# Instance norm on one core: statistics per tile instead of per four tiles, VectorE in program order, six data buffers instead of eleven

## The chip, the core and the metric

The kernel runs on one core of a Trainium2 chip. The metric is the device time of one execution in microseconds (us), lower is better. Each kernel has several timed executions; I quote their median and range. All profiled executions told here are "fast", with the clock granted in full (1.00). A profile also gives a span, from the first to the last work on the core, which is some 1.7 us less than the time of the same execution (1263.8 and 1265.47 us in the changed kernel).

Engine names in the profile: PE is TensorE, PEld its weight loads, DVE is VectorE, ACT is ScalarE, POOL is GpSimd, SP is SyncE; SPq and ACTq are the sequencers that issue DMAs.

## The reference

```python
# x: (8, 64, 32, 64, 64) float32, eps = 1e-5
mean = np.mean(x, axis=(2, 3, 4), keepdims=True)
var  = np.var(x, axis=(2, 3, 4), keepdims=True)
return (x - mean) / np.sqrt(var + eps)
```

There are 512 instances of 131,072 elements. Every element is read once and written once: 268.4 MB in, 268.4 MB out.

## The kernel before

A tile is 128 partitions x 4096 elements of float32, 2 MB in the profile's count (2048 KB), and holds four instances of 32 partitions each; there are 128 tiles. Per tile: a load on SP's queue, eight `bn_stats` and one `bn_aggr` on VectorE. Per batch of T = 4 tiles: a matmul with the selector `sel` sums the 32 partitions of each instance, ScalarE and VectorE make 1/std and -mean/std of them, a matmul with `sel2` spreads the two numbers over the partitions again. Then ScalarE normalises each tile in place and issues its store.

```python
T = 4
data_pool = ctx.enter_context(tc.tile_pool(name="data", bufs=11))
...
for b in range(NB):
    stats = stats_pool.tile([P, T, 2], fp32, name="stats")
    for ti in range(T):
        in_t = data_pool.tile([P, FT], fp32, name="in_t")
        nc.sync.dma_start(out=in_t, in_=x_v[t])
        for s in range(NS):                                  # NS = 8
            nc.vector.bn_stats(out=bnst[:, s, :], in_=in_t[:, s * BS : (s + 1) * BS])
        nc.vector.bn_aggr(out=stats[:, ti, :], in_=bnst)
    ...   # square, add, matmul, scale on ACT, variance, sqrt on ACT, reciprocal,
    ...   # product, matmul, copy to bcast: once for the four tiles
    for ti in range(T):
        nc.scalar.activation(out=in_t, in_=in_t, func=AF.Identity,
                             bias=bcast[:, ti, 1:2], scale=bcast[:, ti, 0:1])
        nc.scalar.dma_start(out=out_v[t], in_=in_t)
```

No engine has a prescribed order: a scheduler arranges each engine's instructions when the kernel is built.

## Time and profile before

| | before |
|---|---|
| time, median (range, runs) | 1317.3 us (1315.9 to 1319.3, 13 runs) |
| span of the profiled execution | 1316.0 us |
| bytes moved, mean rate | 537.05 MB, 408 GB/s |
| rate in undisturbed stretches | 429 to 433 GB/s |
| busy: DVE, ACT | 53%, 38% |

The first parts of the prediction show and read the main lines.

```profile
q14 instruction: 18, 0.15, 0.0%
q8 instruction: 1, 0.02, 0.0%
...
in_t<-in_x_dram SPq DMA_DIRECT2D x128, 2048.0 KB, 16.9
out_dram<-in_t ACTq DMA_DIRECT2D x128, 2048.0 KB, 22.8
```

Instruction traffic looks like nothing: 0.17 MB of 537.

### The profile page before, as it was taken

The page shows a single profiled execution, that of the slowest core. Times are in us where ns is not written, and L with a number is a line of the kernel's source. Part 1 is how long each engine was busy: PE and PEld are TensorE (multiplying, and loading weights), DVE is VectorE, ACT ScalarE, POOL GpSimd, SP SyncE. Part 2 cuts the span into 40 slices and gives each one's busy share as a digit, 9 for nine tenths or more (in the row PEclk, how much of TensorE's full clock was granted, in tenths as well). Part 3 has the DMA queues.
Part 4 walks back from the last instruction along what each step waited for, and adds up shares of the span by engine and source line. Part 5 has one row for each costly group of instructions (what it writes and reads, how often), then busy time and mean ns, then how long its engine had stood idle before and what let it go on. Part 6 is the DMA issues. An engine that isn't in the chain of part 4 may idle for free.

```text
span 1316.0 us, 2530 instructions
## 1 busy us (share of the span) xinstructions
PE 22.7 (2%) x128; PEld 18.4 (1%) x128; DVE 692.6 (53%) x1383; ACT 495.2 (38%) x194; POOL 0.8 (0%) x6
## 2 busy tenths in 40 slices
PE   0000000000000000000000000000000000000000
PEld 0000000000000000000000000000000000000000
DVE  7775546454464545645455454554635546455430
ACT  0431904409054080530805318053180631706345
POOL 0000000000000000000000000000000000000000
DMA  9999999999999999999999999999999999999979
GB/s 396 422 432 429 372 431 395 419 431 380 432 390 421 432 385 432 377 429 430 378 431 385 431 424 385 432 373 432 419 394 432 376 431 408 400 430 373 431 327 399
DMA packets 36883, 537.05 MB, mean 408 GB/s; under 512 B 4096, under 2 KB 4096, under 8 KB 4096
## 3 DMA queue, kind: packets, MB, share of 16 engines
q1 hardware_dynamic: 18432, 268.44, 49.0%
q10 hardware_dynamic: 18432, 268.44, 48.6%
q14 instruction: 18, 0.15, 0.0%
q8 instruction: 1, 0.02, 0.0%
HBM read 268.44 MB, written 268.44 MB: 408 GB/s over the span
## 4 chain that ended last, share of the span: by engine, by line
DMA 60%; ACT 14%; issue 14%; DVE 9%; ACTq 1%; PE 1%; SPq 0%
DMA out_dram<-in_t 38%; DMA in_t<-in_x_dram 22%; ACT in_t L171 14%; DVE bnst L101 7%; ACTq L178 1%; PE psum_b L158 1%; DVE stats L104 1%; ACT std_t L138 0%; DVE bcast L166 0%; DVE bsrc L147 0%; DVE bsrc L148 0%; DVE var_t L135 0%; DVE nm L126 0%; SPq L97 0%; DVE sq_tmp L106 0%
## 5 line engine op out<-in xcount | busy, mean ns | idle before, releaser
L101 DVE BATCH_NORM_STATS2 bnst<-in_t 128x6 f32<-128x512 f32 x1024 | 619.3, 677 | 554.0 <-DMA in_t<-in_x_dram 553.9
L171 ACT ACTIVATE in_t<-in_t,bcast 128x4096 f32<-128x4096 f32 x128 | 479.5, 3793 | 40.3 <-ACT in_t L171 20.3
L123 ACT ACTIVATE sc<-psum_s 4x8 f32<-4x8 f32 x32 | 5.3, 166 | 603.6 <-PE psum_s L114 502.9
L138 ACT ACTIVATE std_t<-var_t,eps_t 4x4 f32<-4x4 f32 x32 | 7.9, 289 | 161.3 <-DVE var_t L135 161.3
L104 DVE BATCH_NORM_AGGREGATE stats<-bnst 128x2 f32<-128x48 f32 x128 | 47.6, 372 | 4.4
L114 PE MATMUL psum_s<-stats,sel 128*4 128x8 f32 x64 | 6.3, 172 | 1067.6 <-DVE stats L109 997.5
L158 PE MATMUL psum_b<-bsrc,sel 4*128 4x8 f32 x64 | 16.4, 361 | 179.8 <-DVE bsrc L148 179.8
L114 PEld LDWEIGHTS psum_s<-stats,sel 128*4 128x4 f32 x64 | 3.6, 83 | 1069.9 <-issue 579.3
L158 PEld LDWEIGHTS psum_b<-bsrc,sel 4*128 4x128 f32 x64 | 14.8, 316 | 181.7 <-DVE bsrc L148 178.5
L166 DVE COPY bcast<-psum_b 128x8 f32<-128x8 f32 x32 | 5.3, 166 | 10.3 <-PE psum_b L158 10.0
L147 DVE RECIPROCAL bsrc<-std_t 4x4 f32<-4x4 f32 x32 | 5.2, 162 | 4.3 <-ACT std_t L138 4.3
L109 DVE TENSOR_TENSOR stats<-stats,sq_tmp 128x4 f32<-128x4 f32 x32 | 5.2, 163 | 1.1
L106 DVE TENSOR_TENSOR sq_tmp<-stats 128x4 f32<-128x4 f32 x32 | 5.2, 163 | 1.1
L148 DVE SCALAR_TENSOR_TENSOR bsrc<-sc,bsrc 4x4 f32<-4x4 f32 x32 | 4.8, 150 | 1.0
L135 DVE TENSOR_TENSOR var_t<-sc,nm 4x4 f32<-4x4 f32 x32 | 3.7, 146 | 0.0
L126 DVE SCALAR_TENSOR_TENSOR nm<-sc 4x4 f32<-4x4 f32 x32 | 2.7, 115 | 0.5 <-ACT sc L123 0.5
L123 ACT ACT_TABLE_LOAD x1 | 1.3, 1283 | 0.8 <-PEq L195 0.8
L138 ACT ACT_TABLE_LOAD x1 | 1.3, 1283 | 0.0
L58 DVE MEMSET sel<- 128x4 f32 x1 | 0.1, 62 | 0.9 <-PEq L195 0.9
L60 DVE MEMSET sel<- 32x1 f32 x4 | 0.2, 59 | 0.1
L64 POOL TENSOR_SCALAR_AFFINE_SELECT sel<-sel 4x128 f32<-4x128 f32 x1 | 0.3, 283 | 0.6 <-DVE sel L63 0.6
L73 POOL TENSOR_SCALAR_AFFINE_SELECT sel<-sel 4x128 f32<-4x128 f32 x1 | 0.3, 282 | 0.1
(6 smaller groups left out, 0.6 us busy)
## 6 DMA issues: line engine op xcount, KB each, us to landing
in_t<-in_x_dram SPq DMA_DIRECT2D x128, 2048.0 KB, 16.9
out_dram<-in_t ACTq DMA_DIRECT2D x128, 2048.0 KB, 22.8
```

Of the source, the lines that this page charges most:

```text
L101: nc.vector.bn_stats(out=bnst[:, s, :], in_=in_t[:, s * BS : (s + 1) * BS])
L104: nc.vector.bn_aggr(out=stats[:, ti, :], in_=bnst)
L106: nc.vector.tensor_mul(out=sq_tmp, in0=stats[:, :, 0], in1=stats[:, :, 0])
L109: nc.vector.tensor_add(out=stats[:, :, 1], in0=stats[:, :, 1], in1=sq_tmp)
L114: nc.tensor.matmul(out=psum_s, lhsT=sel, rhs=stats, start=True, stop=True,)
L123: nc.scalar.mul(out=sc1, in_=psum_s, mul=inv_PG)
L138: nc.scalar.activation(out=std_t, in_=var_t, func=AF.Sqrt, bias=eps_t[0:R, :], scale=1.0,)
L147: nc.vector.reciprocal(out=bsrc[:, :, 0], in_=std_t)
L158: nc.tensor.matmul(out=psum_b, lhsT=sel2, rhs=bsrc, start=True, stop=True,)
L166: nc.vector.tensor_copy(out=bcast, in_=psum_b)
L171: nc.scalar.activation(out=in_t, in_=in_t, func=AF.Identity, bias=bcast[:, ti, 1:2], scale=bcast[:, ti, 0:1],)
L178: nc.scalar.dma_start(out=out_v[t], in_=in_t)
```

## The change

The intent is to let every tile go out as soon as its own statistics are there. The small chain runs once per tile; VectorE keeps program order, tile after tile (a `LAG` of 0: tile t is finished before t+1 begins); and since a tile is held for a shorter time, six data buffers are to suffice. The division by 32 is folded into the constants. Core of the diff, with cuts:

```diff
-    T = 4
+    TAIL_TILES = 0
-    data_pool = ctx.enter_context(tc.tile_pool(name="data", bufs=11))
+    data_pool = ctx.enter_context(tc.tile_pool(name="data", bufs=6))
-    for b in range(NB):
-        stats = stats_pool.tile([P, T, 2], fp32, name="stats")
-        for ti in range(T):
+    def front(t):
         ...                       # load, 8 bn_stats
-            nc.vector.bn_aggr(out=stats[:, ti, :], in_=bnst)
+        nc.vector.bn_aggr(out=stats, in_=bnst)          # stats is [P, 2]
         ...                       # square, add, matmul with sel
-        nc.scalar.mul(out=sc1, in_=psum_s, mul=inv_PG)
+        nc.vector.tensor_copy(out=sc, in_=psum_s)
         ...                       # two operations for the variance
+        return in_t, sc, q2
+    def back(t, in_t, sc, q2):
         ...                       # sqrt, reciprocal, product, matmul with sel2, bcast,
         ...                       # normalise and store this one tile
+    LAG = 0
+    held = {}
+    with tc.manual_schedule(engines={mybir.EngineType.DVE}):
+        for t in range(NT + LAG):
+            if t < NT:
+                held[t] = front(t)
+            if t >= LAG:
+                back(t - LAG, *held.pop(t - LAG))
```

(`TAIL_TILES` would split the last tiles between VectorE and ScalarE; at 0 it does nothing.)

## The prediction

> **What bounds the kernel now.** I read the first page from the top, then the windows, then the waits of the DMA-issuing queues, then the timeline around one dip.
>
> ```profile
> PE 22.7 (2%) x128; PEld 18.4 (1%) x128; DVE 692.6 (53%) x1383; ACT 495.2 (38%) x194; POOL 0.8 (0%) x6
> ...
> DMA  9999999999999999999999999999999999999979
> GB/s 396 422 432 429 372 431 395 419 431 380 432 390 421 432 385 432 377 429 430 378 431 385 431 424 385 432 373 432 419 394 432 376 431 408 400 430 373 431 327 399
> DMA packets 36883, 537.05 MB, mean 408 GB/s; under 512 B 4096, under 2 KB 4096, under 8 KB 4096
> ```
>
> No engine is busy much over half, while the DMA row is full: this is a copy of 268 MB in and 268 MB out with some arithmetic. But the GB/s row is not flat. It sits at 429 to 432 for a while and falls to 372 to 395 at a regular beat; the mean is 408. The busy digits hide that, so I cut the run into stretches of 20 us and, round one dip, of 2 us (columns: stretch, length, busy us of PE, PEld, DVE, ACT, POOL, clock, DMA share, GB/s).
>
> ```profile
> 600.00:620.00 20.00, 0.20 (x2) 0.12 (x2) 10.49 (x21) 0.17 (x1) 0.00 (x0) 1.00 1.01 432
> 620.00:640.00 20.00, 1.02 (x4) 0.93 (x4) 12.88 (x31) 16.23 (x7) 0.00 (x0) 1.00 0.89 350
> 640.00:660.00 20.00, 0.20 (x2) 0.12 (x2) 6.82 (x14) 14.22 (x4) 0.00 (x0) 1.00 1.01 421
> 660.00:680.00 20.00, 0.00 (x0) 0.00 (x0) 10.97 (x21) 0.17 (x1) 0.00 (x0) 1.00 1.00 429
> ```
>
> ```profile
> 624.00:626.00 2.00, 0.00 (x0) 0.00 (x0) 2.00 (x4) 2.00 (x1) 0.00 (x0) 1.00 0.85 360
> 626.00:628.00 2.00, 0.00 (x0) 0.00 (x0) 2.00 (x5) 2.00 (x2) 0.00 (x0) 1.00 0.02 8
> ...
> 638.00:640.00 2.00, 0.00 (x0) 0.00 (x0) 0.00 (x0) 1.53 (x2) 0.00 (x0) 1.00 0.77 213
> 640.00:642.00 2.00, 0.00 (x0) 0.00 (x0) 0.00 (x0) 2.00 (x1) 0.00 (x0) 1.00 1.09 344
> ```
>
> At 626 to 628 us nothing moves at all. ACT is in the middle of normalising and no store has been issued yet; there is no load either, because the load queue waits for stores:
>
> ```profile
> SPq L97 <- DMA out_dram<-in_t: 1164.3, 117, 23.7
> ```
>
> So this is a starvation by buffers. The scheduler let two batches of 4 tiles run together (their small statistics come in pairs, x2 and x4, at 621 to 623 us, and the chain of work repeats every 82 us with 8 tiles in it: loads 598.54, 680.68, 762.60). Eight loaded tiles wait for the last of them, the other 3 of the 11 buffers are filled meanwhile, loads stop, and until the first of the eight has been normalised no store exists. Then comes a phase of stores alone, with a second loss when the loads come back (638 to 642 us, 213 and 344 GB/s). Eight tiles are 8 x 4.194 MB = 33.55 MB; at 431 GB/s, the level of the good stretches, that is 77.9 us, so each 82.0 us period loses about 4.1 us. Some 15.5 such periods lose 64 us. At the end of the run it is worse: the last eight tiles start their stores only after the last load.
>
> ```profile
> 1266.00:1268.00 2.00, 0.20 (x2) 0.12 (x2) 1.53 (x6) 0.04 (x1) 0.00 (x0) 1.00 0.31 131
> 1268.00:1270.00 2.00, 0.85 (x4) 0.86 (x4) 1.06 (x8) 0.63 (x4) 0.00 (x0) 1.00 0.00 0
> 1270.00:1272.00 2.00, 0.16 (x1) 0.07 (x1) 0.17 (x1) 2.00 (x1) 0.00 (x0) 1.00 0.00 0
> 1272.00:1274.00 2.00, 0.00 (x0) 0.00 (x0) 0.00 (x0) 2.00 (x2) 0.00 (x0) 1.00 0.00 0
> ```
>
> That is 7.4 us of silence. 537.05 MB at 431 GB/s are 1246 us; the span is 1316. The 70 us between them are what a better order could win, and no more.
>
> [...] 429 to 433 GB/s in the good stretches, with loads and stores mixed. [...] So I take 431, measured, as the ceiling. [...]
>
> **The change part by part.** I looked at the built order of both kernels too.
>
> 1. Batch of 4 tiles (8 in practice) becomes a batch of 1. A tile's store no longer waits for seven other tiles. It removes the empty 2 us of every period, the phase of stores alone, and the pile of eight stores at the end.
>
> 2. The small operations are done per tile: 128 times instead of 32. On DVE each is 115 to 166 ns in the table of groups; the after kernel has 8 of them per tile (square, add, copy from PSUM, two for the variance, reciprocal, one product, copy of the broadcast), so about 8 x 0.15 = 1.2 us per tile. ACT loses the copy of the sums (166 ns x 32) and gets 128 square roots at 289 ns: 37 us in all against 13. PE doubles nothing that matters.
>
> 3. DVE keeps program order, with no lag: it finishes tile t (statistics, PE, square root on ACT, PE, broadcast) before it begins the statistics of t+1, and waits meanwhile. This is the step that could hurt, so the sum, from the single chain of the first batch (square 29.18, first matmul 29.60 to 29.80, next engine starts 29.84) and the pair at 621 us (square root 621.80, reciprocal 622.12, second matmul 622.53, broadcast 623.16 to 623.33, ACT begins 623.36): square to matmul done 0.65; copy 0.2; two variance operations 0.35; square root to reciprocal 0.32; reciprocal to second matmul 0.41; matmul to broadcast done 0.8. Sum 2.75 us. Ahead of it are eight statistics in 4.85 us and the aggregate in 0.37 (the row of 677 ns per piece counts overlap; eight of them end 4.85 us after the first began). DVE's period: 4.85 + 0.4 + 2.75 = 8.0 us per tile, 128 x 8.0 = 1024 us. The DMA's period is 4.194 MB at 431 GB/s = 9.73 us. DVE keeps 1.7 us in hand in each tile. ACT needs 3.79 + 0.29 + 0.34 for the issue of the store, and it is done with tile t-1 about 4.2 us into DVE's period, before the square root is wanted at 6.4 us.
>
> 4. Buffers 11 to 6. Loads may run at most 6 tiles ahead. By hand: loads land every 4.9 us at first, DVE begins at 8.6 us, the first store is issued near 8.6 + 8.0 + 3.8 = 20.4 us and shares the engines with loads 5 and 6, which hold out to about 42 us; it lands at 33 to 34 us and releases load 7, some 8 us before the load queue would run dry. From there a buffer's round at 9.73 us per tile is 6 x 9.73 = 58 us: load with its wait about 19, compute 8.0 + 4.2 = 12, leaving about 27 us for a store that takes 9.7 when sharing. So about two stores and two loads are always queued, and the DMA never lacks work. 6 is enough because a tile's life outside the DMA is short. ACT's store issue waits for the store four before it (from the built waits), which this leaves alone.
>
> The sum: 1246 us for the bytes; the head, 2.6 us (the first 20 us moved 375 GB/s: 7.5 MB, worth 17.4 us); one loss like that of 638 to 642 us when the stores first join, 1.5; the tail, where the last load lands with two to three stores still queued (10 to 15 us of work at full rate) while its own tile needs 2 + 8.0 + 4.2 = 14 us, so 0 to 3 us of silence, say 1; the last landing 1.7 (in before packets stop at about 1314 of 1316.0). 1246 + 2.6 + 1.5 + 1 + 1.7 = 1252.8 us of span, and the timed runs are 1.3 us over the span: 1254 us, 4.8% below 1317.3.
>
> **The rivals.**
> - DVE becomes the bound, because it now waits for PE and ACT in every tile. For: no lag, and the chain crosses engines four times. Against: 8.0 us against 9.73; it would need 1.7 us more in each tile. If the chain took 5 us instead of 2.75, the time would be 128 x 10.25 = 1312 plus ends: same as before.
> - Six buffers are too few and the two queues run dry in turn. For: the loss at 638 to 642 us shows that it costs some 1.5 us when a queue comes back. If it happened in each tile at half that, 128 x 0.75 = 96 us would put the time at 1350. Against: the round above leaves each queue one transfer in reserve, and in the stretches with both queues at work before (60 to 120 us) the rate holds at 432 to 433.
> - The dips are not starvation but the price of ACT and DVE using the memory beside the DMA, or of turning between reads and writes. Then the dips stay and the time is 1300 to 1317. Against: the empty 2 us have no packet at all, and from 20 to 40 us DVE was busy for 19.67 us at 429 GB/s.
>
> **Range and chances.** The ceiling is measured and hard: nothing under 1246. The sum has few free terms, all small. I take 1247 to 1270; the upper part is for a queue that runs dry now and then. Faster by over 2% means under 1291, which leaves 37 us for errors: 0.95. Within 2%: 0.04, one of the rivals at part strength. Slower: 0.01.
>
> **What would show it.** Right: the GB/s row flat at 428 to 433 in all slices but the first and last; DVE's idle time still mostly on loads, with 1 to 2 us per tile; about 2.8 us between aggregate and broadcast; loads and stores each landing 17 to 27 us after issue; fewer than 5 us without packets at the end. Wrong: DVE idle mostly on PE and ACT with no wait on loads (first rival), slices of 380 to 410 throughout with loads released late by stores (second), or dips at full packet share (third).

## The result, and the profile after

The changed kernel took **1265.64 us** (1265.50 to 1265.92, 8 runs) against 1317.3: ratio 0.9608, 95% interval 0.9599 to 0.9618. A ratio here is the mean time of one kernel's fast runs over that of the other's of the same rounds, so it is not quite the ratio of the medians. It is 3.9% faster; 1254 was predicted, in a range of 1247 to 1270.

The page of the changed kernel, the rows that the prediction showed of before, and the instruction queues:

```profile
PE 99.1 (8%) x512; PEld 75.0 (6%) x512; DVE 823.3 (65%) x2183; ACT 525.3 (42%) x257; POOL 0.8 (0%) x6
...
GB/s 389 431 431 431 431 431 431 430 431 431 429 430 429 431 430 431 430 431 431 430 431 430 431 431 431 431 431 430 431 429 429 428 425 424 427 431 428 427 428 277
DMA packets 36892, 537.15 MB, mean 425 GB/s; under 512 B 4096, under 2 KB 4096, under 8 KB 4096
...
q14 instruction: 24, 0.20, 0.0%
q8 instruction: 4, 0.07, 0.0%
...
in_t<-in_x_dram SPq DMA_DIRECT2D x128, 2048.0 KB, 17.0
out_dram<-in_t ACTq DMA_DIRECT2D x128, 2048.0 KB, 30.2
```

The beat of dips is gone. The row stands at 431 for three quarters of the run. Two things are new: from about the thirty-second slice it sags, mostly to 424 to 428, and the last slice is at 277. A store now lands 30 us after its issue. VectorE has 800 instructions more (x2183 against x1383).

VectorE's loop, from the timeline of one tile (start, length in us, engine, line, operation; in brackets the idle time before it and what ended it):

```profile
642.55 4.85 DVE L91 BATCH_NORM_STATS2 bnst<-in_t 128x6 f32<-128x512 f32 x8 [1.73 <-DMA in_t<-in_x_dram]
...
647.43 0.37 DVE L95 BATCH_NORM_AGGREGATE stats<-bnst 128x2 f32<-128x48 f32 x1
...
650.35 0.16 DVE L158 COPY bcast<-psum_b 128x2 f32<-128x2 f32 x1 [0.67 <-PE psum_b L150]
650.55 3.80 ACT L163 ACTIVATE in_t<-in_t,bcast 128x4096 f32<-128x4096 f32 x1 [1.23 <-DVE bcast L158]
652.26 4.84 DVE L91 BATCH_NORM_STATS2 bnst<-in_t 128x6 f32<-128x512 f32 x8 [1.75 <-DMA in_t<-in_x_dram]
```

VectorE works from 642.55 to 650.51, 7.96 us, then waits 1.75 us for a load: a tile every 9.71 us, the pace of the DMA. ScalarE is done at 654.35, early. So VectorE does not bound the loop. The totals of the waits (us, times, longest) say the same of the whole run:

```profile
DVE bnst L91 <- DMA in_t<-in_x_dram: 230.3, 120, 7.0
```

Where, then, are the 17.5 us between the span of 1263.8 and the 1246.3 that 537.15 MB take at 431 GB/s? Stretches of the run (columns as in the prediction; the last is GB/s):

```profile
0.00:20.00 20.00, 0.74 (x4) 0.58 (x4) 10.34 (x30) 4.99 (x3) 0.77 (x6) 1.00 0.92 375
20.00:40.00 20.00, 2.33 (x12) 1.76 (x12) 15.41 (x46) 8.87 (x6) 0.00 (x0) 1.00 1.01 423
620.00:640.00 20.00, 1.55 (x8) 1.17 (x8) 13.16 (x36) 8.38 (x5) 0.00 (x0) 1.00 1.01 431
1060.00:1080.00 20.00, 1.55 (x8) 1.18 (x8) 13.66 (x36) 8.19 (x4) 0.00 (x0) 1.00 1.01 424
...
1240.00:1260.00 20.00, 1.20 (x6) 0.93 (x6) 6.59 (x18) 7.89 (x3) 0.00 (x0) 1.00 0.63 266
1260.00:1263.80 3.80, 0.00 (x0) 0.00 (x0) 0.00 (x0) 0.00 (x0) 0.00 (x0) 1.00 0.04 17
```

A stretch of length L at rate r loses L x (1 - r/431). The head: 2.6 + 0.4 us. The end: 20 x (1 - 266/431) = 7.7, and 3.8 x (1 - 17/431) = 3.6, together 11.3. The rest is 17.5 - 3.0 - 11.3 = 3.2 us: about 2.2 of them lie in the sagging stretch from 980 to 1240 us (427 GB/s), and 1.0 is the small shortfall between 40 and 980 us (430.5 GB/s). The end in stretches of 2 us:

```profile
1242.00:1244.00 2.00, 0.00 (x0) 0.00 (x0) 1.63 (x3) 2.00 (x1) 0.00 (x0) 1.00 0.19 82
...
1250.00:1252.00 2.00, 0.14 (x1) 0.05 (x1) 0.16 (x1) 1.63 (x1) 0.00 (x0) 1.00 0.10 41
1252.00:1254.00 2.00, 0.00 (x0) 0.00 (x0) 0.00 (x0) 2.00 (x1) 0.00 (x0) 1.00 0.06 25
...
1260.00:1262.00 2.00, 0.00 (x0) 0.00 (x0) 0.00 (x0) 0.00 (x0) 0.00 (x0) 1.00 0.08 33
```

25 to 41 GB/s is not nothing. A full rate of 431 over the page's 16 DMA engines is 27 each, and the column before the rate, the DMA's busy share, has 0.06 to 0.10 where one of sixteen would be 0.06: in these gaps about **one** of the sixteen is at work and the others are idle.

That led to the completion records. Each transfer has sixteen of them (4096 for 256 transfers), and I read each as the part of one of the 16 DMA engines. In this trace what waits for a transfer waits for the sixteenth: fourteen parts of store 121 had landed by 1208.5 us, the last landed at 1225.3, and only at 1225.4 was load 127 issued, which needs its buffer. I took the time from the first to the sixteenth record of a transfer as its *spread* (worked out from the trace's records; the profile's views show only the last landing). Some transfers at the end of the changed kernel, counted from 0, in us after their first part:

```
transfer     13th  14th  15th  16th part, and when that landed
store 121     2.1   2.1   9.3  18.9   1225.3
load  126     1.2   1.3   1.8   5.2   1232.6
store 122     3.4   3.4  10.7  20.2   1235.1
load  127     1.3   1.4   1.9   5.3   1242.3
store 123     3.1   3.1  10.4  18.7   1243.6
store 124     2.0   2.5   6.2  12.6   1248.4
store 125     1.2   1.3   4.9  11.3   1253.2
store 126     0.1   0.1   1.2   7.5   1258.1
store 127     0.1   0.1   0.1   2.6   1262.9
```

In these last transfers fourteen parts land near each other, one is late and one very late. The largest spread in the neighbourhood of a moment, over the run:

```
              100 us  300 us  600 us  900 us  1200 us
before          1.9     1.2     1.3     1.4     1.8
changed         2.1     4.6    11.8    18.1    19.3
```

In before the engines stay together: as I read it, the late one catches up at every empty moment. In the changed kernel the latest part falls behind for good. From store to store it lands 9.71 us later, but 0.8 to 1.0 us more than that at certain packets of the instruction queue q14, 8 KB each: in the middle of the run those at 459.5, 535.2, 607.1, 683.4, 759.6, 833.3 and 907.1 us, every 74 us or so (a few other packets of q14 lie between, off this beat). That is 7.6 tiles, in which VectorE issues 7.6 x 17 = 130 instructions. Experiment 4 below has 1024 VectorE instructions more and 8 packets of q14 more (32 against 24), one for 128. So I read the q14 packets at that beat as the fetches of VectorE's instructions. These steps are not the whole growth of the spread: at other moments the first part runs ahead (at 478 us it lands 8.5 us after that of the store before, where 9.7 is usual), for a reason I do not know. The lag of the second latest part is mostly not explained by fetches: of the packets of q8 (16 KB at 211, 525, 839 and 1156 us, about every 315 us: 32 tiles with 8 PE instructions each, matmuls and weight loads: 256) only the first goes with a step of it (0.6 us). Mostly it falls back by some 0.06 us in every tile.

This became **theory A**: VectorE's instruction fetches all burden the same DMA engine, that engine falls behind by some 0.9 us per fetch, and since a buffer is only free and a tile only loaded when the slowest part has landed, it sets the end. The engine has its sixteenth of the bytes (1246 us at the common rate), starts at 1.8 us, and with 17 fetches (2183 instructions / 128) loses 15 us: 1263, against the last landing at 1262.9. As rivals, **B** in the form that each experiment gives it: six buffers are too few, or the lone last tiles' VectorE chain sets the end, or VectorE's time per tile counts, not its instructions.

### The profile page after: what moved, and what is told of

Same layout as the page of the kernel before. It is cut to its first block, busy times and chain, and to the rows that moved or that the text cites.

```text
span 1263.8 us, 4141 instructions
## 1 busy us (share of the span) xinstructions
PE 99.1 (8%) x512; PEld 75.0 (6%) x512; DVE 823.3 (65%) x2183; ACT 525.3 (42%) x257; POOL 0.8 (0%) x6
## 2 busy tenths in 40 slices
DMA packets 36892, 537.15 MB, mean 425 GB/s; under 512 B 4096, under 2 KB 4096, under 8 KB 4096
## 4 chain that ended last, share of the span: by engine, by line
DMA 75%; DVE 14%; ACT 7%; PE 2%; issue 1%; SPq 0%
DMA out_dram<-in_t 47%; DMA in_t<-in_x_dram 28%; DVE bnst L91 11%; ACT in_t L163 6%; PE psum_b L150 1%; DVE stats L95 1%; ACT std_t L130 1%; PE psum_s L104 0%; DVE stats L99 0%; DVE sq_tmp L98 0%; DVE bcast L158 0%; DVE bsrc L139 0%; DVE sc L112 0%; DVE bsrc L140 0%; DVE q L115 0%
## 5 line engine op out<-in xcount | busy, mean ns | idle before, releaser
L130 ACT ACTIVATE std_t<-q,eps_t 4x1 f32<-4x1 f32 x128 | 37.6, 293 | 569.9 <-DVE q L124 569.9
L104 PE MATMUL psum_s<-stats,sel 128*4 128x2 f32 x256 | 24.6, 166 | 984.9 <-DVE stats L99 984.9
L150 PE MATMUL psum_b<-bsrc,sel 4*128 4x2 f32 x256 | 74.5, 358 | 166.2 <-DVE bsrc L140 166.2
L158 DVE COPY bcast<-psum_b 128x2 f32<-128x2 f32 x128 | 20.4, 159 | 86.5 <-PE psum_b L150 86.5
L150 PEld LDWEIGHTS psum_b<-bsrc,sel 4*128 4x128 f32 x256 | 63.5, 306 | 179.2 <-DVE bsrc L140 177.8
L104 PEld LDWEIGHTS psum_s<-stats,sel 128*4 128x4 f32 x256 | 11.5, 84 | 995.8 <-DVE stats L99 995.8
L139 DVE RECIPROCAL bsrc<-std_t 4x1 f32<-4x1 f32 x128 | 19.3, 151 | 46.2 <-ACT std_t L130 46.2
L112 DVE COPY sc<-psum_s 4x2 f32<-4x2 f32 x128 | 18.9, 148 | 36.6 <-PE psum_s L104 36.6
L99 DVE TENSOR_TENSOR stats<-stats,sq_tmp 128x1 f32<-128x1 f32 x128 | 20.4, 159 | 4.5
L98 DVE TENSOR_TENSOR sq_tmp<-stats 128x1 f32<-128x1 f32 x128 | 20.4, 159 | 4.4
L140 DVE SCALAR_TENSOR_TENSOR bsrc<-sc,bsrc 4x1 f32<-4x1 f32 x128 | 18.9, 147 | 4.4
## 6 DMA issues: line engine op xcount, KB each, us to landing
out_dram<-in_t ACTq DMA_DIRECT2D x128, 2048.0 KB, 30.2
```

The lines of the kernel that those rows point to most:

```text
L98: nc.vector.tensor_mul(out=sq_tmp, in0=stats[:, 0:1], in1=stats[:, 0:1])
L99: nc.vector.tensor_add(out=stats[:, 1:2], in0=stats[:, 1:2], in1=sq_tmp)
L104: nc.tensor.matmul(out=psum_s, lhsT=sel, rhs=stats, start=True, stop=True,)
L112: nc.vector.tensor_copy(out=sc, in_=psum_s)
L130: nc.scalar.activation(out=std_t, in_=q2, func=AF.Sqrt, bias=eps_t[0:R, :], scale=-neg_inv_PG,)
L139: nc.vector.reciprocal(out=bsrc[:, 0:1], in_=std_t)
```

## The experiments

All kernels gave correct results. Ratios are to the kernel before, in the same rounds, with 95% intervals. For comparison the changed kernel: 0.9608 [0.9599, 0.9618].

**1. Which part of the change wins.** The kernel before, batch of 4 and 11 buffers as they were, with nothing but VectorE's order prescribed:

```diff
-    for b in range(NB):
-        ...                           # the whole loop, indented
+    with tc.manual_schedule(engines={mybir.EngineType.DVE}):
+        for b in range(NB):
+            ...
```

> The kernel before with one thing changed: DVE keeps program order, so batches stay at 4 tiles and two no longer merge to 8; 11 buffers as before. If the loss of before came from 8 tiles held together out of 11 buffers (the prediction's account), most of the gain comes without the batch of 1: no empty 2 us in the middle, GB/s flat near 430, a longer tail than in the changed kernel because four stores follow the last load; 1262 to 1275 us. If the batch of 1 itself is what matters, it stays at 1300 to 1317.

Measured: 1260.35 us (1260.10 to 1260.81), ratio 0.957 [0.9557, 0.9583]. So the program order alone, without the batch of 1, wins all of the change and 5 us more. What had cost 57 us was the scheduler's letting two batches run as one; in this kernel's trace the small chain runs once for each four tiles (first matmul at 599.88, the next at 639.69 us). The batch of 4 needs 800 fewer VectorE instructions. Its spread grows too, though later (7.7 us at 900 us, 18.2 at 1200).

**2. More buffers.**

```diff
-    data_pool = ctx.enter_context(tc.tile_pool(name="data", bufs=6))
+    data_pool = ctx.enter_context(tc.tile_pool(name="data", bufs=11))
```

> The changed kernel with 11 data buffers in place of 6, nothing else. In the trace of the changed kernel the sixteenth part of a store (one of the 16 DMA engines) lands 1 us after the first at 35 us and 19 to 20 us after it at 1200 us, and the lag grows in steps of about 0.9 us. Theory A: one DMA engine carries extra work (the small instruction-fetch packets) and is itself full to the end, 2048 packets of data plus some 15 us; then more buffers can't help: 1262 to 1267 us, within 3 us of the changed kernel's 1265.6. Theory B: the 11.5 us lost in the tail are a dependency, too few stores are queued when the last load lands because there are only 6 buffers; then 11 buffers keep the DMA fed to the end and the time falls by 8 to 10 us, to 1255 to 1258.

Measured: 1273.31 us (1273.27 to 1273.46), ratio 0.9668 [0.9655, 0.9681]. Both theories missed: it is *slower* than with 6, by 7.7 us. Its waits (us, times, longest) and stretches:

```profile
ACT std_t L130 <- DMA out_dram<-in_t: 419.2, 93, 5.4
...
DVE bsrc L139 <- ACT std_t L130: 289.2, 128, 24.1
```

```profile
620.00:640.00 20.00, 1.54 (x8) 1.17 (x8) 13.21 (x36) 8.19 (x4) 0.00 (x0) 1.00 1.00 429
1220.00:1240.00 20.00, 2.13 (x10) 1.67 (x10) 16.09 (x43) 11.21 (x6) 0.00 (x0) 1.00 0.68 289
1240.00:1260.00 20.00, 1.87 (x11) 1.39 (x11) 15.91 (x46) 9.36 (x6) 0.00 (x0) 1.00 0.64 272
```

With more buffers the loads run further ahead of the stores. ScalarE's queue then stands still at a store until an earlier store has landed (first line), and loaded tiles pile up before VectorE. The middle of the run is at the full rate. But the last load lands at 1226 us, and what is left are stores alone, one every 7.9 us, as fast as VectorE's chain without lag gives them, while a store by itself takes 2.10 MB / 431 GB/s = 4.9 us (the lone stores at the end of before land 4.9 us apart: 1294.9, 1299.8, 1304.7). Six gaps of some 3 us follow (289 and 272 GB/s). So the buffers only move the pile from the queue to VectorE, and there it drains slowly.

**3. Fewer buffers.**

```diff
-    data_pool = ctx.enter_context(tc.tile_pool(name="data", bufs=6))
+    data_pool = ctx.enter_context(tc.tile_pool(name="data", bufs=4))
```

> The changed kernel with 4 data buffers. By the prediction's round: 4 x 9.73 = 38.9 us; a tile needs 12.2 us of compute, and with both queues busy a load 9.7 and a store 9.7 plus some 1.5 us each for landing: 34.6 us, just enough, but the lag of one DMA engine (20 us by the end with 6 buffers) does not fit any more, so the other engines wait for it: 1264 to 1275 us. If 6 was already the edge, far more: over 1290.

Measured: 1278.91 us (1278.31 to 1282.43), ratio 0.971 [0.9697, 0.9723], 4 us above the range. (The 1.5 us for landing were my estimate; in the changed kernel the first part of the last store lands 6.1 us after its issue, 1.2 more than its bytes take at 431 GB/s.) The rate is 416 to 432 GB/s in nearly every slice: now the queues do run dry a little in each tile. The spread stays under 7.4 us, as I read it because an engine that is far behind stops everybody. Of 4, 6 and 11 buffers, 6 is the best for this loop.

**4. Eight more tiny instructions per tile on VectorE.** They compute nothing of use:

```diff
         nc.vector.tensor_copy(out=bcast, in_=psum_b)
+        nc.vector.tensor_copy(out=junk, in_=bcast[:, 0:1])       # junk is [128, 1]
+        for _ in range(7):
+            nc.vector.memset(junk, 0.0)
```

> The changed kernel with eight more tiny DVE instructions per tile (one copy of 128x1 from the broadcast and seven memsets of 128x1), useless on purpose; results stay right. 1024 more instructions on DVE, about 0.5 to 0.8 us more of DVE per tile, so its period is 8.5 to 8.8 us against the DMA's 9.73: DVE still isn't the bound. Theory A (instruction fetches delay one DMA engine, one fetch of 8 KB per some 128 DVE instructions, 0.9 us each): 8 more fetches, 7 us more: 1270 to 1275 us. Theory B (tail dependency): the last tile's chain is at most 0.8 us longer: 1265 to 1267.

Measured: 1273.59 us (1273.53 to 1273.65), ratio 0.967 [0.9657, 0.9683]. That is 8.0 us for 1024 instructions, or 8 fetches (32 packets of q14 against 24), as A has it. VectorE would still have had time: 895.7 us busy of 1272.

**5. The same eight on GpSimd.**

```diff
+        nc.gpsimd.tensor_copy(out=junk, in_=bcast[:, 0:1])
+        for _ in range(7):
+            nc.gpsimd.memset(junk, 0.0)
```

> The same eight tiny instructions per tile on GpSimd in place of DVE. Theory A with one fetch engine for each issuing engine: GpSimd has hardly any instructions of its own, so its fetches load a DMA engine that is not the slowest: within 2 us of 1265.6. If all fetches ran through one DMA engine it would be as with DVE: 1270 to 1275. Theory B: 1265 to 1266.

Measured: 1267.30 us (1267.27 to 1267.33), ratio 0.9622 [0.9609, 0.9635]. The instruction queues of the two kernels, VectorE's first, then GpSimd's:

```profile
q14 instruction: 32, 0.26, 0.0%
```

```profile
q14 instruction: 34, 0.28, 0.1%
```

As many fetches more (8 and 10 over the 24 of the changed kernel), and yet 1.7 us instead of 8.0. By their beats, nine of the ten are GpSimd's (every 138 us) and one is VectorE's own, whose packets come every 69 us here, 18 in place of 17; at some 0.9 us that one could be half of the 1.7. The latest part falls back only slightly further (20.7 us at 900 us, against 18.1 in the changed kernel), the second latest more (16.4 against 11.5), but in every tile and not at GpSimd's packets. As I read it, it is not the amount of instruction traffic that counts but on which DMA engine it lies; below the packets themselves show that GpSimd's lie on another than VectorE's.

**6. Two small instructions fewer per tile.** One `scalar_tensor_tensor` makes mean x mean + variance, another the variance over the instance, with 1/32 put into `sel`:

```diff
-        nc.vector.tensor_mul(out=sq_tmp, in0=stats[:, 0:1], in1=stats[:, 0:1])
-        nc.vector.tensor_add(out=stats[:, 1:2], in0=stats[:, 1:2], in1=sq_tmp)
+        nc.vector.scalar_tensor_tensor(out=stats[:, 1:2], in0=stats[:, 0:1],
+            scalar=stats[:, 0:1], in1=stats[:, 1:2], op0=ALU.mult, op1=ALU.add)
...          # likewise q1 and q2 become one
```

> The changed kernel with two small DVE instructions fewer per tile (the square and the sum in one, the variance in one), the same arithmetic and 6 buffers: 256 DVE instructions fewer, two fetches of 8 KB. Theory A (DVE's instruction fetches hold up one DMA engine, 0.9 us each; confirmed by +8.0 us for 1024 more DVE instructions and +1.7 us for as many on GpSimd): 1.8 to 2.5 us less, 1263 to 1264. Theory B (only the dependency at the end counts): the last chain is 0.4 us shorter, 1265.

Measured: 1264.01 us (1263.85 to 1265.62), ratio 0.9594 [0.9581, 0.9607]. Its q14 has 22 packets, two fewer than the changed kernel. The direction and size fit; the intervals overlap, so by itself this shows little.

**7. VectorE's time or its instruction count?** Experiment 4 adds both. First, one large useless instruction per tile, 0.6 us of VectorE:

```diff
+    junk = const_pool.tile([P, 6], fp32, name="junk")
...
         nc.vector.tensor_copy(out=bcast, in_=psum_b)
+        nc.vector.bn_stats(out=junk, in_=in_t[:, 0:BS])
```

> Control for the eight tiny DVE instructions: the changed kernel with one useless instruction per tile of about the same DVE time (one more partial statistic of 128x512, 0.6 us). Theory A (the number of instructions counts): 128 more, one fetch, 1265.5 to 1267.5. If DVE's time, or the 0.6 us that it adds to each tile, was what cost 8.0 us before: 1272 to 1274.

Measured: 1269.18 us, but scattered from 1267.05 to 1273.92 (5 runs); ratio 0.9631 [0.9617, 0.9645]. That lies between the two expectations and decides nothing. So I added the same instruction and saved another (the first half of experiment 6): 17 instructions per tile as in the changed kernel, about 0.5 us more VectorE time.

> The changed kernel with a useless bn_stats of 128x512 added per tile (about 0.55 us of VectorE) and one small operation saved (square and add done by one scalar_tensor_tensor): 17 VectorE instructions per tile as in the changed kernel, but about 0.45 us more VectorE time per tile. Theory A (what costs is the number of instructions, by the fetches): 1265 to 1267, as changed. Rival (VectorE's time per tile counts, because it delays the store of each tile): about 1269 to 1272, as the kernel with the useless operation added outright, which came to 1269.2 with a wide scatter. If A holds and the scatter is gone, that kernel's 3.5 us belong to its one instruction more and to scatter; if it comes to 1269 or more, VectorE's time has a part in it as well.

Measured: 1266.35 us (1265.95 to 1267.07), ratio 0.9617 [0.9604, 0.963]; VectorE busy 887.3 us against 823.3. 64 us more of VectorE's work cost 0.7 us, where experiment 4's 72 us, in 1024 instructions, cost 8.0. So VectorE's time does not explain experiment 4's 8.0 us. It leaves the previous kernel's extra 3.5 us unexplained, of which one more fetch would be about 1. Why that kernel scatters by 7 us I do not know; its profile is of its slowest run, whose latest part was up to 26.7 us behind. In that run, from about 890 us on, the latest part takes up to 10.4 us from store to store without a fetch, where 9.71 is usual, and 54, 99 and 98 packets of 16 KB in 100 us take over 0.78 us (from 900, 1000 and 1100 us), where the changed kernel has 16, 40 and 20. So that part of the slowest run is not fetches.

**8. A shorter tail.** The last two tiles are normalised half by VectorE, half by ScalarE, and stored as halves.

```diff
-    TAIL_TILES = 0
+    TAIL_TILES = 2
```

> The changed kernel with the last two tiles normalised in halves, one half by DVE and one by ACT, each stored at once. The last chain gets about 2 us shorter. Theory A: the slow DMA engine works without a break to the end (its part of the last store lands 2.5 us after the others, which have waited), so nothing or at most 1 us is won: 1264.5 to 1266. Theory B: 2 to 3 us less, 1262.5 to 1263.5.

Measured: 1265.93 us (1265.87 to 1266.33), ratio 0.9607 [0.9594, 0.962]: nothing won. Fifteen parts of the last store land at 1257.9 us, 2.5 us earlier than in the changed kernel (1260.5), as intended; the latest lands 5.7 us after the first, at 1263.5, against 1262.9 in the changed kernel. Stretches of this kernel's end:

```profile
1250.00:1252.00 2.00, 0.00 (x0) 0.00 (x0) 1.50 (x2) 1.81 (x1) 0.00 (x0) 1.00 0.11 45
...
1260.00:1262.00 2.00, 0.00 (x0) 0.00 (x0) 0.00 (x0) 0.00 (x0) 0.00 (x0) 1.00 0.07 29
```

Most engines' idle time at the end is slack, as I read it: the late one works through it and has the end to itself (29 GB/s at 1260 to 1262 us, about one engine's 27).

**9. The statistics with two instructions instead of nine.** VectorE sums the tile in one `reduce_sum`, ScalarE makes the sum of squares in one activation with `accum_out`; 6 VectorE instructions per tile in place of 17. Both engines in program order; the first version copies the broadcast of tile t-1 after the sum of tile t:

```diff
-        for s in range(NS):
-            nc.vector.bn_stats(out=bnst[:, s, :], in_=in_t[:, s * BS : (s + 1) * BS])
-        nc.vector.bn_aggr(out=stats, in_=bnst)
-        ...                                         # square and add
+        nc.vector.reduce_sum(out=stats[:, 0:1], in_=in_t, axis=mybir.AxisListType.X)
+        nc.scalar.activation(out=scratch, in_=in_t, func=AF.Square,
+                             accum_out=stats[:, 1:2])
...
+        for t in range(NT + 1):       # sqrt of t-1; front(t); broadcast, normalise, store t-1
```

> The statistics taken another way: one DVE sum and one ACT sum of squares over a tile's 4096 columns in place of eight partial statistics, an aggregate and a product on DVE; 6 buffers, batch of 1, DVE and ACT in program order. DVE has 6 instructions per tile in place of 17, some 6 fetches over the run in place of 16; ACT has some 4 us more per tile, 8.5 of the 9.73 us. Theory A: the slowest DMA engine gets some 9 us less: 1254 to 1258 us, with the spread of a store's 16 parts at the end under 10 us. If the engines drift apart for another reason than instructions, or if only the dependency at the end counts, 1263 to 1266. If ACT becomes the bound: over 1270.

Measured: 1307.59 us (1307.54 to 1307.65), ratio 0.9922 [0.9909, 0.9936]: a miss by 50 us. The waits:

```profile
DVE bsrc L130 <- ACT std_t L121: 582.0, 128, 4.9
...
ACT in_t L158 <- DVE bcast L153: 250.3, 128, 2.0
```

VectorE waits for ScalarE's root and ScalarE for VectorE's broadcast copy, which stands behind the sum of 4.40 us. From the timeline: root at 608.16, sum from 608.75 to 613.15, broadcast at 613.85, normalising from 614.02 to 617.82, next root at 618.24. A loop of 10.08 us, longer than the DMA's 9.7: my own order had made the rival "VectorE waits for others" true.

**10. The same, with the broadcast ahead of the sum.** Only the order of two pieces changes (told in comments here, not in the lines of the code):

```diff
         for t in range(NT + 1):
-            # root(t-1); front(t); broadcast copy, normalise, store of t-1
+            # root(t-1) with its broadcast copy; front(t); normalise, store of t-1
```

> The kernel with one DVE sum and one ACT sum of squares per tile again, 6 buffers, but with the broadcast of tile t-1 finished before the sum of tile t begins. In the first form it came after that sum, and the loop square root, sum, broadcast, normalising took 10.07 us per tile, over the DMA's 9.73. Now ACT needs 0.3 + 3.8 + 3.8 + 0.4 = 8.3 us per tile and DVE about 7. Theory A (one fetch of instructions per some 128, about 0.9 us of one DMA engine each; DVE now 775 instructions, 6 fetches in place of 17): 1254 to 1259 us. If the engines' drift had nothing to do with the number of DVE instructions: 1263 to 1266. If the normalising of a tile, which now waits for the load of the next one, needs more than 6 buffers: 1262 to 1275.

Measured: **1257.15 us** (1256.89 to 1257.29), ratio 0.9542 [0.9529, 0.9555]. This beats both kernels. Its page:

```profile
PE 98.8 (8%) x512; PEld 78.4 (6%) x512; DVE 669.3 (53%) x775; ACT 986.7 (79%) x514; POOL 0.8 (0%) x6
...
GB/s 387 431 432 430 431 432 431 431 431 431 431 431 431 432 430 429 433 431 429 432 430 431 432 431 432 429 431 432 431 431 432 431 431 432 431 430 432 430 431 349
```

With 775 instructions VectorE fetches 6 times (8 KB each, at a beat of about 207 us). The rate does not sag, the largest spread at 1200 us is 10.9, and the last slice is at 349 instead of 277.

**11. One buffer more for it.**

```diff
-    data_pool = ctx.enter_context(tc.tile_pool(name="data", bufs=6))
+    data_pool = ctx.enter_context(tc.tile_pool(name="data", bufs=7))
```

> The same with 7 data buffers, since a tile is now held until the next one has landed. Theory A: 1253 to 1258 us, at most 2 us below the one with 6; a number below 1258 beats every kernel so far.

Measured: 1257.41 us (1257.12 to 1257.73), ratio 0.9544 [0.9531, 0.9557]: no gain.

**Together.** The theory's arithmetic, 1246 + 1.8 + 0.9 us for each 128 VectorE instructions, against the spans. Fetches are instructions over 128: against the changed kernel's 24 packets of q14 there are 8 more for 1024 instructions more (4), 2 fewer for 256 fewer (6), 1 more for 128 more (7, first). Left out are the kernels with another bound: 4 and 11 buffers, and the sums with the late broadcast.

| kernel | VectorE instructions | fetches | 1247.8 + 0.9 x fetches | span measured |
|---|---|---|---|---|
| sums, broadcast early (10) | 775 | 6.1 | 1253.3 | 1255.4 |
| batch of 4, in order (1) | 1383 | 10.8 | 1257.5 | 1259.0 |
| two fewer (6) | 1927 | 15.1 | 1261.4 | 1263.9, its slowest run |
| changed | 2183 | 17.1 | 1263.2 | 1263.8 |
| time only (7, second) | 2183 | 17.1 | 1263.2 | 1264.3 |
| short tail (8) | 2183 | 17.1 | 1263.2 | 1264.6 |
| eight on GpSimd (5) | 2183 | 17.1 | 1263.2 | 1265.5 |
| one large more (7, first) | 2311 | 18.1 | 1264.1 | 1272.2, its slowest run |
| eight more (4) | 3207 | 25.1 | 1270.4 | 1271.9 |

From the medians, 0.8 us per fetch between the first kernel and the changed one ((1265.6 - 1257.2) / 11.0) and 1.0 between the changed one and the one with eight more (8.0 / 8.0). The 0.9 is an estimate from the steps of the latest part; the sixteen such steps after the first 30 us of the changed kernel add up to 15.1 us, 0.94 each.

**The packets themselves.** The records name no DMA engine, but they show which packets share one. A packet of 16 KB takes 0.611 us where nothing disturbs it, and another starts 0.607 us after it, again and again, so the packets can be strung into sixteen chains (worked out from the trace's records; no view shows them). The chain with the fetch of 459.47 us in the changed kernel, in us from the start of that fetch:

```
 start   length
 -0.61    0.61   data
  0.00    0.31   fetch of 8 KB, q14
  0.31    1.25   data
  1.55    0.61   data
```

The data packet behind the fetch takes 1.25 us instead of 0.61. With the fetch's own 0.31 the chain loses 0.94 us, which is the step. Following this chain on to its next packet that closes a store (4 bytes), the *latest* part of that store lands 0.44 us after it starts. So it is, within 0.43 to 0.47 us, after 14 of the 17 fetches of VectorE's beat; at two more, two chains start packets within a few ns of each other and one of the two fits, and at the first, at 28.7 us, the engines have not drifted apart yet (the transfers that land from 32 to 45 us have a spread of 1.0 to 1.3 us). VectorE's fetches thus lie on the engine that lands last. In experiment 5 GpSimd's nine fetches lie on another chain, at six of the nine that of the third latest part. In experiment 10 VectorE's six fetches lie, late in the run, on the chain of the second latest part: another engine lands last there. Its end is then no longer set by VectorE's fetches, and the 0.8 us per fetch, for which it is one of the two ends, is too low if anything.

What stays open: why the data packet behind a fetch takes twice as long; why the second latest part falls back a little in every tile; and the scatter in experiment 7. No experiment moved VectorE's fetches to another DMA engine, which would be the direct proof that they alone set the end; I know of no way to do so.

## Why the prediction was right or wrong

**The bound, and the cure of the dips: right.** The DMA bounds both kernels, the dips were starvation, and 431 GB/s holds when they are gone. That the two merged batches were the cause is shown by experiment 1: un-merging them is enough. The batch of 1, which the prediction put first, is not needed for it.

**The small operations: right in VectorE's time, incomplete in kind.** VectorE became 130.7 us busier, 1.0 us per tile. The prediction counted the 800 instructions only as time on VectorE; their fetches were in no term.

**VectorE's period: right.** 8.0 us predicted, 7.96 measured, 1.75 us waiting for loads where 1.7 were left over; 2.8 us from the end of the aggregate to that of the broadcast (647.80 to 650.51 is 2.71). The first rival is false for this kernel (and experiment 9 shows what it looks like when true).

**The buffers: right in number, wrong in the picture.** "So about two stores and two loads are always queued, and the DMA never lacks work" holds to the end only for the latest engine; for all sixteen together it holds to about 980 us, going by the rate. Store 121 was issued at 1195.0; its first part landed at 1206.4, 11 us later, its last at 1225.3, 30 us later. The prediction's own sign, landings within 17 to 27 us, was broken by the stores at 30.2: the one sign on the page that something was amiss. The prediction's 9.7 us for a store beside a load is what the trace has: by the packet records of before, loads move 216 GB/s and stores 215 from 60 to 80 us, and 2.10 MB at 216 GB/s take 9.7 us.

**The sum: the step that failed is the tail.**

| term, us | predicted | measured |
|---|---|---|
| the bytes at 431 GB/s | 1246 | 1246.3 |
| head | 2.6 | 2.6 |
| one switch when the stores join | 1.5 | 0.4 |
| middle | 0 | 3.2 |
| tail and last landing | 1 + 1.7 | 11.3 |
| span | 1252.8 | 1263.8 |

The tail was set as "the last load lands with two to three stores still queued", so "0 to 3 us of silence, say 1". In fact the last load's latest part landed at 1242.3, and by then most engines had nothing queued at all (82 GB/s in 1242 to 1244). The load had been issued late, at 1225.4, since its buffer came free only when the latest part of store 121 landed. Its own 11.8 us through VectorE and ScalarE (1242.37 to 1254.20; 8.0 + 4.2 predicted) then lay bare for most engines. Of the middle's 3.2 us I put the late 2.2 down to the same cause: late in the run even the fast engines run short of work now and then, because the slow one frees the buffers too late. That is argued from the place of the sag, not tested by itself, though it is gone where VectorE has 6 instructions (experiment 10). The assumption under both terms, never written down, was that sixteen engines share every transfer evenly to the end. That 1265.6 us still lies in the range of 1247 to 1270 is in part luck: its upper part was kept for "a queue that runs dry now and then", not for engines that drift apart. And the 1.3 us from span to time compared the median with the span of another execution; within one execution it is 1.7 (1265.47 and 1263.8).

**The rivals.** Six buffers too few: false at 6, true at 4, and 11 are worse. Contention of reads and writes: false, the middle runs at 431.

## What to carry to other kernels

In these kernels, bound by DMA, the time is that of the slowest of the DMA engines (in the changed kernel the latest part of the last store lands at 1262.9 of 1263.8 us), and removing the idle moments, as I read the spreads (1.4 us before, 18.1 after, at 900 us), also removed the time in which a slow one caught up. Look at the first and the last part of a transfer's landing, not only at the mean rate; stretches at a sixteenth of the full rate near the end were the sign here. The number of VectorE's instructions was a cost of its own (8.0 us for 1024 in experiment 4), though the engine was idle a third of the time, and more buffers made it worse where they only let loads run ahead of stores (1273.3 us with 11, 1265.6 with 6). And before a batch is taken apart, try to keep the scheduler from merging two.
